# Up projections of a squared-ReLU MLP: a 512- and a 256-column matmul per weight tile against three of 256 columns

## The chip, the core and the metric

One NeuronCore of a Trainium2 chip runs the kernel. TensorE (PE) multiplies: it loads a stationary 128x128 tile (PEld in the profile) and streams a moving operand past it into PSUM, here in accumulators of one bank, 512 float32 columns. VectorE (DVE), ScalarE (ACT) and GpSimd (POOL) work beside it, and SyncE (SP) issues the weight transfers. The metric is the device time of one execution in microseconds; lower is better.

## What is computed

Two decoder layers over 256 tokens of width 2048, in float32. Layer 0 mixes tokens by differential attention, layer 1 by a gated linear recurrence; each is followed by a squared-ReLU MLP of hidden width 8192 and a gated per-layer embedding. The change touches the MLP:

```python
def sqrelu_mlp(xn, w_up, w_down):
    return jnp.square(jax.nn.relu(xn @ w_up)) @ w_down

for i in range(DEPTH):                                   # two layers
    h = h + mix                                          # attention or recurrence
    h = h + sqrelu_mlp(rmsnorm(h, g_mlp[i]), w_up[i], w_down[i])
    ple_gate = jax.nn.sigmoid(rmsnorm(h, g_ple[i]) @ w_ple_gate[i])
    h = h + ple_gate * (p[i] @ w_ple_proj[i])
```

## The kernel before

Every matrix product is made from float32 operands split into two float32r parts, `hi` and `lo`, and sums three of the four partial products: hi·hi, hi·lo and lo·hi. All products go through one weight stream, `stream(groups)`. A group is one product of [256 tokens, 512 columns] over `nk` k-tiles of 128. Its weights come in chunks of four k-tiles (one 1 MB transfer on SP's queue, three buffers); a chunk is cut into subs of two k-tiles, and each sub is split by one ACT cast (`w_hi`, L255) and one DVE subtraction (`w_lo`, L256) into one of four buffers, up to three subs ahead of the matmuls. Small work that hangs on a group (transposes, norms) is deferred by a number of subs and emitted between the matmuls.

In most groups the activations are stationary and 512 weight columns move: `mm3` (L249 to L251) issues three matmuls of 512 columns for each k-tile and each half of the tokens. The gate products of layer 1, the attention scores and the attention outputs use `mm3` too, with 256 or 128 moving columns.

The up projections of the MLP are transposed (`flip`): the result is wanted as [hidden, tokens], so a 128x128 weight tile is stationary and the 256 tokens move. The moving operand is a `Wide` tile (`x.both`), with the `hi` and the `lo` part of a k-tile side by side, 512 columns in all. For each weight tile (a k-tile `k`, one of four column blocks `f`) line L391 issues two matmuls. One has `w_hi` stationary and moves all 512 columns: columns 0 to 255 of the accumulator `acc[f]` receive hi·hi, columns 256 to 511 hi·lo. The other has `w_lo` stationary and moves the 256 `hi` columns into columns 0 to 255. So one group has four accumulators of a full bank, out of six in the pool. When the group is done, `up_evict` adds the two halves: an ACT copy of the right half (L644), a DVE addition (L645), then relu and square in one DVE instruction over two blocks (L646), and a split of the result into `big` tiles (L255, L256), the operand of the down projection.

One layer's MLP has 8 chunks of 1024 hidden columns. `up(c)` is two groups (2 x 16 k-tiles x 4 blocks = 128 weight tiles), `down(c)` four groups (4 x 8 k-tiles x 2 token halves x 3 = 192 matmuls of 512 columns). The order is up(0), up(1), down(0), up(2), down(1), and so on, so that a down projection never follows directly on the eviction that it needs, but for the last. Over both layers there are 16 x 128 = 2048 weight tiles.

Of the kernel before, what the change touches and what calls it, by code (L numbers as in the profile page):

```python
# [11 lines left out]
AF = mybir.ActivationFunctionType  # L12
# [30 lines left out]
class Chunk:  # L43
    """Up to KC k-tiles of one weight column block, moved by one DMA."""

# [5 lines left out]
class Sub:  # L51
    """SK k-tiles of a chunk, split into two float32r parts."""

# [6 lines left out]
class Group:  # L60
    """One product over nk k-tiles: [256 tokens, 512 columns], or its transpose where flip is set."""

# [11 lines left out]
def trunk_kernel(ctx: ExitStack, tc, a, out):  # L74
# [7 lines left out]
    def t4(shape, dtype=F32):  # L82
        """4 KiB a partition"""
        return wk.tile(shape, dtype, tag="t4", name="t4", bufs=3)
# [10 lines left out]
    def big(shape, dtype=F32):  # L95
        """8 KiB a partition"""
        return wk.tile(shape, dtype, tag="big", name="big", bufs=4)
# [12 lines left out]

# [1 line left out]
    state = {"tick": 0}  # L112
# [13 lines left out]

# [1 line left out]
    h = cp.tile([P, NT, D], F32, name="h")  # L128
# [66 lines left out]
    def lam_setup():  # L195
        """lambda of the differential attention, the same on every partition"""
        lamv = t2([P, 4, DK])
        for i, nm in enumerate(("lam_q1", "lam_k1", "lam_q2", "lam_k2")):
            nc.gpsimd.dma_start(lamv[:, i], a[nm][0].partition_broadcast(P))

        def finish():
            lamm = t1([P, 2, DK])
            nc.vector.tensor_tensor(lamm, lamv[:, 0::2], lamv[:, 1::2], op=ALU.mult)
            lams = sm.tile([P, 2], F32, name="lams", bufs=1)
            nc.vector.tensor_reduce(lams, lamm, axis=AX.X, op=ALU.add)
            lame = sm.tile([P, 2], F32, name="lame", bufs=1)
            nc.scalar.activation(lame, lams, AF.Exp)
            nc.vector.tensor_tensor(neg_lam, lame[:, 1:2], lame[:, 0:1], op=ALU.subtract)
            nc.vector.tensor_scalar(neg_lam, neg_lam, LAM0, None, op0=ALU.subtract)

        defer(4, finish)

    def mask_setup():
        """-(query - key) where the key is visible, else a huge negative number"""
        nc.gpsimd.iota(
            mtab, pattern=[[-P, NT], [1, SEQ]], base=0, channel_multiplier=-1, allow_small_or_imprecise_dtypes=True
        )
        nc.gpsimd.affine_select(
            mtab, mtab, pattern=[[P, NT], [-1, SEQ]], compare_op=ALU.is_ge, fill=NEG, base=0, channel_multiplier=1
        )  # L220

    # 8 * softplus(-lam): log1p(u) = 2 atanh(u / (2 + u)) with u = exp(-|lam|)
    sp8 = cp.tile([P, 16], F32, name="sp8")
# [22 lines left out]

# [1 line left out]
    def mm3(ps, lh, ll, rh, rl, start, stop):  # L248
# [4 lines left out]
    def split(hi, lo, src):  # L253
        """src = hi + lo exactly, each part of float32r's 12 significant bits."""
        nc.scalar.copy(hi, src)  # L255
        nc.vector.tensor_tensor(lo, src, hi.bitcast(F32), op=ALU.subtract)  # L256
# [5 lines left out]
    def rstd(ss, n, width, name):  # L262
        """(ss / width + EPS) ** -0.5 of [P, n]"""
        m = sm.tile([P, n], F32, name=name + "_m")
        nc.gpsimd.tensor_scalar(m, ss, 1.0 / width, EPS, op0=ALU.mult, op1=ALU.add)
        r = sm.tile([P, n], F32, name=name + "_r")
        nc.gpsimd.tensor_tensor(r, m, mhalf[:, :n], op=ALU.pow)
        return r

    def x32(shape):  # L270
        """32 KiB a partition"""
        return xp.tile(shape, F32R, tag="x32", name="x32")

    class Operand:
        """A split [k, token] operand of nk k-tiles."""

# [6 lines left out]
    class Wide(Operand):  # L283
        """Both parts of a k-tile side by side: one [k, 512] moving operand."""

# [4 lines left out]
    class Norm(Wide):  # L290
        """The rmsnorm of h as a transposed, split operand; the row factor r goes onto the products."""

# [37 lines left out]

# [1 line left out]
    def stream(groups):  # L332
# [34 lines left out]
        for g in groups:  # L367
            acc = [psum([P, NB]) for _ in range(4 if g.flip else NT)]
            kt = 0
            for i, s in enumerate(g.subs):  # L370
                load_to(cidx[id(s.chunk)] + W_RAW - 1)
                if i in g.pre:
                    g.pre[i](split_to)
                split_to(j + W_SPLIT - 1)
                j += 1
                if s.own is not None:
                    continue
                if g.flip:
                    x = g.lhs()
                    for f in range(4):  # L380
                        fs = slice(f * P, (f + 1) * P)
                        for kk in range(SK):
                            k = kt + kk
                            parts = [
                                (acc[f][:, :SEQ], s.lo[:, kk, fs], x.hi[:, k]),
                                (acc[f], s.hi[:, kk, fs], x.both[:, k].rearrange("p a t -> p (a t)")),
                            ]
                            if k == 0:
                                parts.reverse()
                            for n, (o, lh, rh) in enumerate(parts):  # L390
                                nc.tensor.matmul(  # L391
                                    o, lhsT=lh, rhs=rh, start=k == 0 and n == 0, stop=k == g.nk - 1 and n == 1
                                )
                else:
                    for t in range(NT):
                        for kk in range(SK):
                            k = kt + kk
                            lh, ll = g.lhs(k, t)
                            mm3(acc[t], lh, ll, s.hi[:, kk], s.lo[:, kk], k == 0, k == g.nk - 1)
                kt += SK  # L400
                state["tick"] += 1
                run_due()
            g.evict(acc)
# [3 lines left out]

# [1 line left out]
    pT = {}  # L409
# [14 lines left out]

# [1 line left out]
    n0 = Norm(G_MIX)  # L426
# [41 lines left out]
    def softmax(ps, heads, t, nk):  # L468
        """attn = softmax(c = 0) - lam * softmax(c = 1) of [P, heads, 2, nk] scores"""
        n = len(heads)  # L470
# [122 lines left out]
    def residual_evict(nb, norm, scale=None):  # L593
        """h += product; the last contribution to this block feeds the next norm."""

        def evict(acc):
            add_to_h(acc, nb, scale)
            if norm is not None:
                norm().feed(nb)

        return evict
# [22 lines left out]

# [1 line left out]
    FC = 1024  # L626
# [3 lines left out]
    def mlp(l, norm_in, norm_out):  # L630
        hid = {}

        def up_evict(c, half):
            """relu(.) ** 2 of a transposed product; the row factor squared goes onto the next product"""

            def evict(acc):
                if half == 0:
                    hid[c] = Operand(big([P, FKT, SEQ], F32R), big([P, FKT, SEQ], F32R))
                for b in range(2):
                    u = t2([P, 2, SEQ])  # L640
                    for i in range(2):
                        ps = acc[2 * b + i]
                        other = t1([P, SEQ])
                        nc.scalar.copy(other, ps[:, SEQ:])  # L644
                        nc.vector.tensor_tensor(u[:, i], ps[:, :SEQ], other, op=ALU.add)  # L645
                    nc.vector.scalar_tensor_tensor(u, in0=u, scalar=0.0, in1=u, op0=ALU.max, op1=ALU.mult)  # L646
                    ks = slice(half * 4 + 2 * b, half * 4 + 2 * b + 2)
# [24 lines left out]

# [1 line left out]
    def ple(l, norm_in, norm_out):  # L674
# [49 lines left out]

# [1 line left out]
    w_in = a["w_in_rec"][0]  # L726
# [9 lines left out]
    def gate_weights():  # L736
        """They lie in the k-tiles of yT that come last."""
        w = yT().both[:, 8:16]
        return w[:, :, 0], w[:, :, 1]
# [64 lines left out]
    def recur(half):  # L804
        """a = exp(-s r), b = sqrt(1 - a^2) i x with 1 - a^2 = tanh(s r) (1 + a^2); then the scan"""

# [66 lines left out]
    def gate_chunk(nb):  # L873
        """The gate weights of 512 channels: they go through the weight stream's loads and splits."""
        ch = Chunk(None, KC)
# [34 lines left out]

    # the first group takes x as it comes
    first = groups[0]
# [64 lines left out]
```

## Time and profile before

| | us |
|---|---|
| median of 3 runs | 2328.12 |
| lowest and highest of them | 2327.57 and 2328.15 |
| span of the profiled execution | 2326.8 |
| PE busy | 2308.8 (99%) |
| DVE busy, ACT busy | 1424.6 (61%), 1193.6 (51%) |
| matmuls, and weight loads | 11467 each |

The span runs from the first to the last instruction of the profiled execution. It is 1.3 us below the median. Matmuls are pipelined: the duration of one (0.28 us with 256 columns) is longer than the distance to the next, so what a matmul occupies is read from the distance between two starts, or from a stretch of known length divided by the count of matmuls in it. "This matmul's pace" below means that distance.

### The profile page before, as it was taken

How to read it: one execution, taken by the hardware profiler on the slowest of the kernel's cores; microseconds unless marked ns; L12 is line 12 of the kernel's file. 1: busy time of each engine (PE TensorE's matmuls, PEld its weight loads, DVE VectorE, ACT ScalarE, POOL GpSimd, SP SyncE). 2: the span in 40 equal slices, each digit the busy share in tenths (PEclk: the TensorE clock that was granted, in tenths of full speed). 3: DMA queues.
4: the chain of work that ended last, by engine and by line, in shares of the span. 5: the costliest groups of instructions: out<-in, count | busy, mean ns of one | idle time of the engine just before them, and what ended most of it. 6: DMA issues, size and time to landing. Idle time of an engine off the chain costs nothing.

```text
span 2326.8 us, 28564 instructions
## 1 busy us (share of the span) xinstructions
PE 2308.8 (99%) x11467; PEld 1946.9 (84%) x11467; DVE 1424.6 (61%) x1704; ACT 1193.6 (51%) x1594; POOL 44.7 (2%) x79
## 2 busy tenths in 40 slices
PE   8999999999999999999999999999999999999999
PEld 6888888888888888888888887888888888888887
DVE  6676655565565665566566767566565555565654
ACT  6555554444444444444558887454444444444453
POOL 2100000000000000000000000000000000000000
PEclk9999999999999999999999999999999999999999
DMA  7454555555565655655566565556565565555554
GB/s 241 163 185 163 165 179 181 185 195 189 191 197 184 198 188 192 196 185 181 189 193 219 187 212 181 181 182 198 184 197 190 191 197 184 198 189 191 177 199 148
DMA packets 225396, 438.95 MB, mean 189 GB/s; under 512 B 7582, under 2 KB 16416, under 8 KB 225264
## 3 DMA queue, kind: packets, MB, share of 16 engines
q1 hardware_dynamic: 224608, 436.24, 57.3%
q8 instruction: 89, 1.46, 0.3%
q0 software_dynamic: 608, 0.89, 0.2%
q14 instruction: 43, 0.35, 0.0%
q10 hardware_dynamic: 48, 0.02, 0.0%
HBM read 435.01 MB, written 2.10 MB: 188 GB/s over the span
## 4 chain that ended last, share of the span: by engine, by line
PE 94%; DVE 2%; ACT 2%; DMA 1%; issue 1%; SPq 0%; POOL 0%; DVEq 0%; ACTq 0%
PE acc L391 31%; PE acc L251 21%; PE acc L249 20%; PE acc L250 20%; PE tp L317 1%; DVE w_lo L256 1%; ACT w_hi L255 1%; DMA w_raw<-in_w_gate_x_dram 0%; DVE t L770 0%; DMA h<-in_x_dram 0%; PE tp L458 0%; DVE big L827 0%; ACT L810 0%; SPq L351 0%; ACT L788 0%
## 5 line engine op out<-in xcount | busy, mean ns | idle before, releaser
L256 DVE TENSOR_TENSOR w_lo<-w_raw,w_hi 128x1024 fp32r<-128x1024 f32 x808 | 987.4, 1224 | 781.4 <-ACT w_hi L255 779.9
L255 ACT CAST w_hi<-w_raw 128x1024 fp32r<-128x1024 f32 x808 | 849.0, 1052 | 979.8 <-PE acc L251 605.7
L391 PE MATMUL acc<-x,w_hi 128*128 128x512 f32 x2048 | 704.8, 394 | 0.0
L391 PE MATMUL acc<-x,w_lo 128*128 128x256 f32 x2048 | 547.8, 278 | 0.0
L249 PE MATMUL acc<-w_hi,x 128*128 128x512 f32 x1152 | 457.1, 397 | 0.0
L250 PE MATMUL acc<-w_lo,x 128*128 128x512 f32 x1152 | 450.2, 391 | 1.9 <-DVE w_lo L256 1.8
L251 PE MATMUL acc<-w_hi,x 128*128 128x512 f32 x1152 | 450.5, 391 | 0.0
L391 PEld LDWEIGHTS acc<-x,w_hi 128*128 128x128 f32 x2048 | 376.0, 188 | 78.6
L249 PE MATMUL acc<-w_hi,big 128*128 128x512 f32 x1024 | 399.7, 390 | 0.0
L251 PE MATMUL acc<-w_hi,big 128*128 128x512 f32 x1024 | 398.6, 389 | 0.0
L250 PE MATMUL acc<-w_lo,big 128*128 128x512 f32 x1024 | 398.4, 389 | 0.0
L391 PEld LDWEIGHTS acc<-x,w_lo 128*128 128x128 f32 x2048 | 384.7, 188 | 11.2
L251 PEld LDWEIGHTS acc<-w_hi,x 128*128 128x128 f32 x1152 | 216.8, 188 | 46.8 <-DVE x L256 0.2
L250 PEld LDWEIGHTS acc<-w_lo,x 128*128 128x128 f32 x1152 | 217.2, 189 | 45.0 <-DVE w_lo L256 3.0
L249 PEld LDWEIGHTS acc<-w_hi,x 128*128 128x128 f32 x1152 | 216.8, 188 | 41.7
L251 PEld LDWEIGHTS acc<-w_hi,big 128*128 128x128 f32 x1024 | 192.2, 188 | 40.3
L250 PEld LDWEIGHTS acc<-w_lo,big 128*128 128x128 f32 x1024 | 192.3, 188 | 39.8
L249 PEld LDWEIGHTS acc<-w_hi,big 128*128 128x128 f32 x1024 | 192.2, 188 | 39.0
L589 DVE SCALAR_TENSOR_TENSOR h<-acc,n_r,h 128x512 f32<-128x512 f32 x128 | 89.9, 744 | 0.0
L644 ACT COPY t<-acc 128x256 f32<-128x256 f32 x128 | 47.5, 371 | 22.8 <-PE acc L391 20.6
L259 ACT ACTIVATE x<-tp,cols_a 128x256 fp32r<-128x256 f32 (+1 forms) x72 | 35.7, 496 | 39.5 <-DVE x L260 39.5
L260 DVE SCALAR_TENSOR_TENSOR x<-tp,cols_a,x 128x256 fp32r<-128x256 f32 (+1 forms) x72 | 36.8, 511 | 18.8 <-ACT x L259 18.8
(173 smaller groups left out, 1064.2 us busy)
## 6 DMA issues: line engine op xcount, KB each, us to landing
w_raw<-in_w_up_dram SPq DMA_DIRECT2D x128, 1024.0 KB, 5.2
w_raw<-in_w_down_dram SPq DMA_DIRECT2D x128, 1024.0 KB, 5.1
w_raw<-in_w_qkv_dram SPq DMA_DIRECT2D x47, 1024.0 KB, 5.2
w_raw<-in_w_ple_gate_dram SPq DMA_DIRECT2D x32, 1024.0 KB, 5.2
w_raw<-in_w_in_rec_dram SPq DMA_DIRECT2D x32, 1024.0 KB, 5.5
w_raw<-in_w_o_attn_dram SPq DMA_DIRECT2D x16, 1024.0 KB, 5.2
w_raw<-in_w_o_rec_dram SPq DMA_DIRECT2D x16, 1024.0 KB, 5.1
w_raw<-in_w_ple_proj_dram SPq DMA_DIRECT2D x8, 512.0 KB, 3.7
```

Source lines behind the costliest of these rows:

```text
L249: nc.tensor.matmul(ps, lhsT=lh, rhs=rh, start=start, stop=False)
L250: nc.tensor.matmul(ps, lhsT=lh, rhs=rl, start=False, stop=False)
L251: nc.tensor.matmul(ps, lhsT=ll, rhs=rh, start=False, stop=stop)
L255: nc.scalar.copy(hi, src)
L256: nc.vector.tensor_tensor(lo, src, hi.bitcast(F32), op=ALU.subtract)
L259: nc.scalar.activation(hi, src, AF.Copy, scale=scale)
L260: nc.vector.scalar_tensor_tensor(lo, in0=src, scalar=scale, in1=hi.bitcast(F32), op0=ALU.mult, op1=ALU.subtract)
L317: nc.tensor.transpose(tp[:, i, t * P : (t + 1) * P], h[:, t, (k0 + i) * P : (k0 + i + 1) * P], ident)
L391: nc.tensor.matmul(o, lhsT=lh, rhs=rh, start=k == 0 and n == 0, stop=k == g.nk - 1 and n == 1)
L589: nc.vector.scalar_tensor_tensor(hb, in0=acc[t], scalar=scale()[:, t : t + 1], in1=hb, op0=ALU.mult, op1=ALU.add)
L644: nc.scalar.copy(other, ps[:, SEQ:])
```

## The change

In flip groups each weight tile gets three matmuls of 256 columns: `w_hi` with the `hi` tokens, `w_hi` with the `lo` tokens, `w_lo` with the `hi` tokens, all three into the same 256 columns. Two column blocks share one bank (`acc[f // 2][:, f % 2]`), so a group has two accumulators in place of four. Only the first matmul into a bank carries the start flag. The eviction has no halves to add: ACT applies relu to both blocks of a bank at once, and DVE multiplies that by the accumulator. The diff also drops comments and docstrings, which is not shown; L391 becomes L392, and L644 to L646 become L643 and L644.

```diff
-            acc = [psum([P, NB]) for _ in range(4 if g.flip else NT)]
+            acc = [psum([P, 2, SEQ]) if g.flip else psum([P, NB]) for _ in range(NT)]
...
                     for f in range(4):
                         fs = slice(f * P, (f + 1) * P)
+                        o = acc[f // 2][:, f % 2]
                         for kk in range(SK):
                             k = kt + kk
                             parts = [
-                                (acc[f][:, :SEQ], s.lo[:, kk, fs], x.hi[:, k]),
-                                (acc[f], s.hi[:, kk, fs], x.both[:, k].rearrange("p a t -> p (a t)")),
+                                (s.hi[:, kk, fs], x.hi[:, k]),
+                                (s.hi[:, kk, fs], x.lo[:, k]),
+                                (s.lo[:, kk, fs], x.hi[:, k]),
                             ]
-                            if k == 0:
-                                parts.reverse()
-                            for n, (o, lh, rh) in enumerate(parts):
+                            for n, (lh, rh) in enumerate(parts):
                                 nc.tensor.matmul(
-                                    o, lhsT=lh, rhs=rh, start=k == 0 and n == 0, stop=k == g.nk - 1 and n == 1
+                                    o, lhsT=lh, rhs=rh, start=k == 0 and n == 0 and f % 2 == 0,
+                                    stop=k == g.nk - 1 and n == 2, skip_group_check=True,
                                 )
...
                 for b in range(2):
                     u = t2([P, 2, SEQ])
-                    for i in range(2):
-                        ps = acc[2 * b + i]
-                        other = t1([P, SEQ])
-                        nc.scalar.copy(other, ps[:, SEQ:])
-                        nc.vector.tensor_tensor(u[:, i], ps[:, :SEQ], other, op=ALU.add)
-                    nc.vector.scalar_tensor_tensor(u, in0=u, scalar=0.0, in1=u, op0=ALU.max, op1=ALU.mult)
+                    nc.scalar.activation(u, acc[b], AF.Relu)
+                    nc.vector.tensor_tensor(u, u, acc[b], op=ALU.mult)
```

On PE, where the first up projection of layer 0 follows the last matmuls of the attention's output projection, the program before has these instructions (`x_2943` is the normed, split input of the MLP, `x_2244` the attention output):

```order
L250 MATMUL acc<-w_lo,x_2244 128x512
L251 MATMUL acc<-w_hi,x_2244 128x512
L391 MATMUL acc<-x_2943,w_hi 128x512
L391 MATMUL acc<-x_2943,w_lo 128x256 x2
L391 MATMUL acc<-x_2943,w_hi 128x512 x2
```

And the changed one, at the same place:

```order
L250 MATMUL acc<-w_lo,x_2244 128x512
L251 MATMUL acc<-w_hi,x_2244 128x512
L392 MATMUL acc<-x_2943,w_hi 128x256 x2
L392 MATMUL acc<-x_2943,w_lo 128x256
L392 MATMUL acc<-x_2943,w_hi 128x256 x2
```

The last two rows of each repeat from there on: per weight tile one matmul of 512 and one of 256 columns before, three of 256 now. The places of the groups among one another are the same.

On ACT, at the end of the first up group, the eviction before (`t_3635` and `t_3645` are the two work tiles, `t_3636` to `t_3649` the copied halves):

```order
L255 CAST w_hi<-w_raw 128x1024 x5
L644 COPY t_3636<-acc 128x256
L644 COPY t_3639<-acc 128x256
L644 COPY t_3646<-acc 128x256
L644 COPY t_3649<-acc 128x256
L255 CAST w_hi<-w_raw 128x1024
L255 CAST big<-t_3635 128x512
L255 CAST w_hi<-w_raw 128x1024
L255 CAST big<-t_3645 128x512
```

And in the changed program:

```order
L255 CAST w_hi<-w_raw 128x1024 x5
L643 ACTIVATE t_3697<-acc 128x512
L255 CAST w_hi<-w_raw 128x1024
L255 CAST big<-t_3697 128x512
L643 ACTIVATE t_3702<-acc 128x512
L255 CAST w_hi<-w_raw 128x1024
L255 CAST big<-t_3702 128x512
```

Four copies of 256 columns became two relus of 512, and the weight casts (`w_hi`) that stood behind all four now stand one behind each relu.

## Rows read from the trace of the kernel before

**Rows 1.** The page: busy time, granted clock in 40 slices, chain that ended last.

```profile
PE 2308.8 (99%) x11467; PEld 1946.9 (84%) x11467; DVE 1424.6 (61%) x1704; ACT 1193.6 (51%) x1594; POOL 44.7 (2%) x79
...
PEclk9999999999999999999999999999999999999999
...
PE 94%; DVE 2%; ACT 2%; DMA 1%; issue 1%; SPq 0%; POOL 0%; DVEq 0%; ACTq 0%
PE acc L391 31%; PE acc L251 21%; PE acc L249 20%; PE acc L250 20%; PE tp L317 1%; DVE w_lo L256 1%; ACT w_hi L255 1%; DMA w_raw<-in_w_gate_x_dram 0%; DVE t L770 0%; DMA h<-in_x_dram 0%; PE tp L458 0%; DVE big L827 0%; ACT L810 0%; SPq L351 0%; ACT L788 0%
```

**Rows 2.** The chain in order of time: start us, us, what; three up stretches.

```profile
410.34 83.64 PE acc L391 x480
537.50 44.40 PE acc L391 x256
...
1649.24 44.40 PE acc L391 x256
```

**Rows 3.** Who waited for whom: us in total, times, longest us.

```profile
ACT w_hi L255 <- PE acc L391: 350.8, 218, 1.8
...
ACT t L644 <- PE acc L391: 20.6, 64, 0.3
```

**Rows 4.** Busy by stretch: one down(c), then one up(c); us and (xinstructions).

```profile
493.97:537.50 43.53, 43.53 (x194) 36.04 (x193) 27.16 (x30) 18.29 (x19) 0.00 (x0) 1.00 0.59 192
537.50:581.90 44.40, 44.40 (x258) 38.80 (x257) 24.63 (x28) 20.28 (x25) 0.00 (x0) 1.00 0.59 192
```

**Rows 5.** The page's groups: up matmuls, and loads of L249 and L250.

```profile
L391 PE MATMUL acc<-x,w_hi 128*128 128x512 f32 x2048 | 704.8, 394 | 0.0
L391 PE MATMUL acc<-x,w_lo 128*128 128x256 f32 x2048 | 547.8, 278 | 0.0
...
L250 PEld LDWEIGHTS acc<-w_lo,x 128*128 128x128 f32 x1152 | 217.2, 189 | 45.0 <-DVE w_lo L256 3.0
L249 PEld LDWEIGHTS acc<-w_hi,x 128*128 128x128 f32 x1152 | 216.8, 188 | 41.7
```

**Rows 6.** Timeline of PE in layer 1: a gate product, 256 columns, stationary weights.

```profile
1252.72 0.28 PE L249 MATMUL acc<-v,x 128*128 128x256 f32 x1
...
1254.13 0.39 PE L249 MATMUL acc<-w_hi,x 128*128 128x512 f32 x1
```

**Rows 7.** Timeline of PE in the attention: scores with 256 columns.

```profile
80.44 0.28 PE L251 MATMUL acc<-x 128*128 128x256 f32 x1
...
80.92 0.40 PE L249 MATMUL acc<-w_hi,x 128*128 128x512 f32 x1
```

**Rows 8.** Timeline of PE in the attention: output product, 256 columns, behind transposes.

```profile
242.36 0.28 PE L250 MATMUL acc<-v,big 128*128 128x256 f32 x1
...
243.61 0.39 PE L249 MATMUL acc<-w_hi,x 128*128 128x512 f32 x1
```

**Rows 9.** Timeline of PE in the attention: scores with 128 columns.

```profile
76.14 0.28 PE L250 MATMUL acc<-x 128*128 128x128 f32 x1
...
77.26 0.28 PE L251 MATMUL acc<-x 128*128 128x128 f32 x1
```

**Rows 10.** Groups of ACT and DVE at evictions: busy us, mean ns, idle before.

```profile
L644 ACT COPY t<-acc 128x256 f32<-128x256 f32 x128 | 47.5, 371 | 22.8 <-PE acc L391 20.6
L435 ACT ACTIVATE t<-acc,n_r 128x512 f32<-128x512 f32 x16 | 10.9, 684 | 1.9 <-PE acc L251 1.5
...
L645 DVE TENSOR_TENSOR t<-acc,t 128x256 f32<-128x256 f32 x128 | 47.9, 416 | 0.0
L646 DVE SCALAR_TENSOR_TENSOR t<-t 128x512 f32<-128x512 f32 x64 | 43.6, 682 | 0.0
...
L587 DVE TENSOR_TENSOR h<-h,acc 128x512 f32<-128x512 f32 x16 | 10.2, 680 | 0.0
```

**Rows 11.** Timeline of ACT at the end of an up group.

```profile
559.74 0.37 ACT L644 COPY t<-acc 128x256 f32<-128x256 f32 x1 [0.32 <-PE acc L391]
560.00 1.06 ACT L255 CAST w_hi<-w_raw 128x1024 fp32r<-128x1024 f32 x1
...
565.30 1.05 ACT L255 CAST w_hi<-w_raw 128x1024 fp32r<-128x1024 f32 x1 [1.10 <-PE acc L391]
```

## Prediction

> **What bounds the kernel now.** Read first the busy shares and the chain that ended last [rows 1]. PE is busy 99% of the span and carries 94% of the chain; the up matmuls of L391 alone carry 31% of it. The granted clock is full in all 40 slices. Read next the chain in order of time [rows 2]: an up(c) is one unbroken piece of 44.40 us with 256 matmuls of L391 and nothing of another engine in it. There are six such pieces a layer, and before them one of 83.64 us with 480 matmuls, which is most of up(0) and up(1). Then the list of waits [rows 3]: where L391 stands there, it is the one waited for. ACT's weight casts wait 350.8 us for it, because they run ahead and want a free buffer, and no row has PE waiting in the MLP. So in the up stages PE's own pace is the time, and a matmul added or shortened there moves the end by what it adds or saves. The up stages are where the change acts; DVE is busy 24.63 of 44.40 us there and ACT 20.28 [rows 4].
>
> **What PE pays per weight tile before.** One up(c) is 128 weight tiles in 44.40 us [rows 4], so a tile costs 44.40 / 128 = 346.9 ns, for one matmul of 512 and one of 256 columns. One down(c) is 192 matmuls of 512 columns in 43.53 us [rows 4], so one of 512 columns takes 226.7 ns. If the 512-column matmul of an up tile costs the same, the 256-column one beside it costs 346.9 - 226.7 = 120.2 ns, which is more than half of 226.7 (113.4). Read as a price per column and one per matmul, 512 columns at 226.7 and 256 at 120.2 differ by 106.5 ns, so 256 columns cost 106.5 ns and every matmul, with the load that goes with it, costs 13.7 ns beside. The work in columns is 768 a tile before and after; what the change adds is one more matmul and one more load a tile.
>
> **Does every matmul have a load of its own?** Yes by the page's counts: L249 and L250 run one behind the other with the same stationary tile and still have 1152 loads each [rows 5]. So the two matmuls with `w_hi` will load it twice, and PE goes from two loads and two matmuls a tile to three and three.
>
> **The price of three.** The first estimate is 3 x 120.2 = 360.6 ns a tile, 13.7 more than 346.9. The trace has three other places with runs of 256-column matmuls, each with its own load. The gate products are the closest in form: stationary weights, moving activations, three matmuls a tile, half a bank as accumulator. From 1252.72 to 1254.13 there are 12 steps in 1.41 us, 117.5 ns each [rows 6], so a tile would cost 352.5, 5.6 more. The scores move a tile from the same kind of buffer as the up stage: 4 steps from 80.44 to 80.92, 120.0 ns [rows 7]. An attention output product that starts right behind transposes shows 11 steps from 242.36 to 243.61, 113.6 ns [rows 8]. So the extra per tile lies between -6.1 ns (3 x 113.6 = 340.8) and +13.7 ns, with the two steady cases at +5.6 and +13.1. I take +13.7, because it comes from the very tiles in question (`w_hi` and `w_lo` stationary, `x` moving, in the same buffers) and the scores agree with it; the gates and the output products move a tile of another pool. Halving the columns again does not go much lower: with 128 columns 10 steps from 76.14 to 77.26 take 112 ns each [rows 9]. That row says that below some width the load, and no longer the columns, sets the pace, and 256 columns are already near it. It speaks against a cheap third matmul.
>
> Sum on PE: 2048 tiles x 13.7 ns = +28.1 us; at the gates' pace 2048 x 5.6 = +11.5 us.
>
> The Trainium skill bears on this, and against the rows ("TensorE: Matmul & The Clock Gate", section Back-to-back issue gap): at full clock the gap is the columns divided by 2.4 GHz plus 2.5 ns, and weight loads are given no share in that formula. By it the extra matmul would cost 2.5 ns a tile, an estimate of 5 us in all. The 226.7 ns of a 512-column step [rows 4] stand against the 215.8 that it gives, so here the row decides.
>
> **The rest of the change, on ACT and DVE.** Per up group ACT drops four copies of 371 ns and gains two relus of 512 columns out of PSUM, for which the nearest row is an ACT pass over 128x512 out of PSUM, 684 ns [rows 10]: 1.48 us against 1.37. DVE drops four additions of 416 ns and two passes of 682 ns, 3.03 us, and gains two multiplications of 128x512 with one operand in PSUM, nearest row 680 ns: 1.36 us [rows 10]. Both engines idle half of the stage, and nobody on the chain waits for them, so I cost the 1.7 us that DVE saves per group at nothing. The cover is PE's own stretch: an up group lasts 22.2 us, and the split tiles are read by a down projection that starts a whole up(c) later. Only behind the last chunk of each layer does down(6) alone, 43.5 us, lie between; that covers it too. The new order puts a weight cast behind each relu, where before the casts stood behind all four copies. The first relu waits for two blocks, the second for all four, so the second is released where the fourth copy was, by 559.74 in the stretch shown, and the next cast began at 560.00; the one at 565.30 waited 1.10 us for a buffer that PE still held [rows 11]. The casts run against the buffers, not against PE. The two casts behind the relus start at most a relu's length later than now, and the buffers are three subs (8.3 us) ahead, so this too costs nothing; if that cover were gone it would be under a microsecond in each of 32 groups. The accumulators take two banks of six in place of four, so no group waits for a bank that it did not wait for before. Transfers and SP's queue keep their order and have more time.
>
> **Sum.** The profiled execution has a span of 2326.8 us and the median of the runs is 1.3 us above it. 2326.8 + 28.1 = 2354.9 by span, and 2356 as the median. With the gates' pace it is 2326.8 + 11.5 + 1.3 = 2339.6. About 0.2% (4.7 us) is what a measurement of this kernel can tell from no change.
>
> **The rivals.**
> First, faster: PE settles in the 113.6 ns rhythm of the output product [rows 8]. A tile then costs 340.8 and the kernel 2048 x 6.1 = 12.5 us less, 2315.6. It decides as soon as the pace is under 346.9 / 3 = 115.6 ns. For it: that row exists, and its stationary and moving tiles look like any others. Against: it stands only behind transposes, and the up stages follow 512-column matmuls, as the gates and scores of [rows 6, 7] do. 5%.
> Second, little change: the third matmul costs almost nothing beside its columns, a pace of 115 to 116.4 ns and a time of 2323.5 to 2332.8. For it: the split into a price per column and one per matmul rests on a subtraction, and some of the 13.7 ns may belong to columns. Against: no steady row lies in that gap. 6%. The page's formula above is the same idea at +2.5 ns a tile, 2048 x 2.5 = 5.1 us and 2333.2, just outside; as a mechanism of this kernel it needs a pace of 116.5 ns, which no row shows. 3%.
> Third, much slower: PE cannot be fed that fast for long. Before, an up stage takes four PE instructions in 346.9 ns, 86.7 ns each; now six in 360.6, 60.1 each. The rows show such a rate (112 / 2 = 56 ns in [rows 9]) for 12 matmuls at a time, never for the 384 of an up(c). If the steady rate of instructions were 65 ns, a tile would cost 390 and the kernel 2048 x 43 = 88 us more, 2416. It decides from 60 ns on. For it: nothing in the trace bounds the rate in a long run under 86.7. Against: no step in the bursts lengthens towards their end. 8%.
> That the change does not do what it says (the second load of `w_hi` is left out) is excluded as far as the counts of [rows 5] go; I give it nothing of its own.
>
> **How the numbers follow.** The forecast, slower by the extra load and matmul at a pace between 117.5 and 120.2 ns, has 78%: 2339.6 to 2356.1, with the upper end likelier. The range widens this by 4 us below and 8 us above, for a pace some ns off and for a wait or two at the evictions: 2336 to 2364. Outside it lie the rivals, 22% before counting that the range's edges take in a little of them. Faster by over 0.2%: 5%. Within 0.2%: 6%. Slower by over 0.2%: 78 + 3 + 8 = 89%.
>
> **What would show it.** In the profile after, an up(c) stretch in the chain should be one piece of 46.2 us (45.1 at the gates' pace) with 384 matmuls, and the down stretches should still take 43.5. Starts of the up matmuls should lie 120 ns apart throughout, with PE waiting for nobody. If the stretch is 43.6 us, the first rival holds; if it is 48 us or more with no waits, the third. If ACT or DVE appears in the chain inside the MLP, my claim that the eviction is covered is wrong.

## The result, and the profile after

The changed kernel takes 2353.65 us (median of 4 runs, 2352.7 to 2353.88), against 2327.85 us for the kernel before in the same comparison (2327.08 to 2328.15). The ratio is 1.011, with a 95% interval of 1.0095 to 1.0124: 25.8 us, 1.1% slower. The forecast was 2356, with a range of 2336 to 2364.

The page of the changed kernel has PE at 99% of the span, as before [rows 1], but with 2048 more matmuls and loads (13515 for 11467) and with 25.7 us more of PE's time, while DVE and ACT have less to do:

```profile
span 2350.9 us, 32627 instructions
...
PE 2334.5 (99%) x13515; PEld 2062.4 (88%) x13515; DVE 1384.3 (59%) x1576; ACT 1182.4 (50%) x1530; POOL 44.6 (2%) x79
...
PEclk9999999999999999999999999999999999999999
```

The chain in order of time, layer 1, whose pieces answer to [rows 2] (start us, us, what):

```profile
1526.50 2.87 PE acc L392 x24
1529.81 2.88 PE acc L392 x24
1533.12 86.39 PE acc L392 x720
1663.06 46.07 PE acc L392 x384
1752.67 46.07 PE acc L392 x384
```

An up(c) is still one unbroken piece of PE, now 46.07 us for 44.40, with 384 matmuls for 256: 120.0 ns each, 359.9 a tile for 346.9. The busy times by stretch answer to [rows 4]; the first is a down(c), the second the up(c) behind it, in the same columns (us, then PE, PEld, DVE, ACT, POOL, and behind them the granted clock, the share of the DMA engines and GB/s):

```profile
495.39:538.94 43.55, 43.55 (x195) 36.06 (x194) 25.68 (x27) 18.39 (x19) 0.00 (x0) 1.00 0.58 189
538.94:585.01 46.07, 46.07 (x386) 46.07 (x384) 23.61 (x23) 19.49 (x21) 0.00 (x0) 1.00 0.57 187
```

The down stretch takes 43.55 us for 43.53, unchanged. In the up stretch a weight load is now in flight all the time, 46.07 of 46.07 us for 38.80 of 44.40 before: with a load under every 256 columns no moment is left without one. The granted clock is 1.00 in both stretches, as before, so it has no part in the difference.

What the stages gained adds up. In each layer the 240 tiles of the first long piece went from 83.64 to 86.39 us (+2.75), six up(c) from 44.40 to 46.07 (+1.67 each), and the 16 tiles between the first transposes from 2.78 + 2.80 to 2.87 + 2.88 (+0.17; read for before in layer 0). That is 12.9 us a layer and 25.9 for both, against 25.8 between the medians. The spans of the two profiled executions differ by 24.1. Of the 1.8 us between, 1.3 lie ahead of the first up matmul, which started at 403.7 us and now at 402.4, in a part of the program that is the same in both; I take that for scatter between executions.

### The profile page after: what moved, and what is told of

It reads as the page before. It is cut to its first block, busy times and chain, and to the rows that moved or that the text cites. A ratio compares the mean times of both kernels' runs of the same rounds, so it can differ in the third digit from the quotient of the medians.

```text
span 2350.9 us, 32627 instructions
## 1 busy us (share of the span) xinstructions
PE 2334.5 (99%) x13515; PEld 2062.4 (88%) x13515; DVE 1384.3 (59%) x1576; ACT 1182.4 (50%) x1530; POOL 44.6 (2%) x79
## 5 line engine op out<-in xcount | busy, mean ns | idle before, releaser
L392 PE MATMUL acc<-x,w_hi 128*128 128x256 f32 x4096 | 738.2, 283 | 0.0
L392 PEld LDWEIGHTS acc<-x,w_hi 128*128 128x128 f32 x4096 | 640.2, 192 | 1.1
L392 PE MATMUL acc<-x,w_lo 128*128 128x256 f32 x2048 | 580.2, 283 | 0.0
L249 PE MATMUL acc<-w_hi,x 128*128 128x512 f32 x1152 | 457.3, 397 | 0.0
L250 PE MATMUL acc<-w_lo,x 128*128 128x512 f32 x1152 | 450.0, 391 | 1.4 <-DVE w_lo L256 1.3
L249 PE MATMUL acc<-w_hi,big 128*128 128x512 f32 x1024 | 400.1, 391 | 0.0
L250 PE MATMUL acc<-w_lo,big 128*128 128x512 f32 x1024 | 398.8, 389 | 0.0
L392 PEld LDWEIGHTS acc<-x,w_lo 128*128 128x128 f32 x2048 | 393.5, 192 | 0.0
L250 PEld LDWEIGHTS acc<-w_lo,x 128*128 128x128 f32 x1152 | 217.1, 188 | 44.2 <-DVE w_lo L256 2.5
L249 PEld LDWEIGHTS acc<-w_hi,x 128*128 128x128 f32 x1152 | 216.8, 188 | 41.6 <-ACT x L259 0.3
L251 PEld LDWEIGHTS acc<-w_hi,big 128*128 128x128 f32 x1024 | 192.3, 188 | 40.2
L249 PEld LDWEIGHTS acc<-w_hi,big 128*128 128x128 f32 x1024 | 192.4, 188 | 39.1
L250 PEld LDWEIGHTS acc<-w_lo,big 128*128 128x128 f32 x1024 | 192.4, 188 | 39.0
L643 ACT ACTIVATE t<-acc 128x512 f32<-128x512 f32 x64 | 38.1, 595 | 16.4 <-PE acc L392 16.4
```

Source lines behind the costliest of these rows:

```text
L249: nc.tensor.matmul(ps, lhsT=lh, rhs=rh, start=start, stop=False)
L250: nc.tensor.matmul(ps, lhsT=lh, rhs=rl, start=False, stop=False)
L251: nc.tensor.matmul(ps, lhsT=ll, rhs=rh, start=False, stop=stop)
L392: nc.tensor.matmul(o, lhsT=lh, rhs=rh, start=k == 0 and n == 0 and f % 2 == 0, stop=k == g.nk - 1 and n == 2, skip_group_check=True,)
L643: nc.scalar.activation(u, acc[b], AF.Relu)
```

## The experiments

My theory: the extra load and matmul on PE, at 120 ns for each 256-column matmul, are the whole of the 25.8 us. The rivals were a share of the eviction or of the two-bank accumulators, a price that depends on which tile is loaded, and the gates' pace of 117.5 ns, whose cause the prediction had left open.

### Three short matmuls with the old accumulators and the old eviction

```diff
-                                (acc[f][:, :SEQ], s.lo[:, kk, fs], x.hi[:, k]),
-                                (acc[f], s.hi[:, kk, fs], x.both[:, k].rearrange("p a t -> p (a t)")),
+                                (acc[f][:, :SEQ], s.hi[:, kk, fs], x.hi[:, k]),
+                                (acc[f][:, SEQ:], s.hi[:, kk, fs], x.lo[:, k]),
+                                (acc[f][:, :SEQ], s.lo[:, kk, fs], x.hi[:, k]),
...
```

> The kernel before with one thing changed: the 512-column matmul of an up tile is two of 256, into the left and the right half of the old full-bank accumulator. Four accumulators a group and the old eviction stay. My theory (the third load and matmul on PE are the whole of it, 120 ns each): an up(c) of 46.1 us with 384 matmuls, and 2328 + 2048 x 13.1 ns = 2354.7, the same as the changed kernel within 1.5 us. Rival (the shared bank or the lighter eviction gives or takes a part): the up(c) differs from 46.07 us or the time differs from 2353.7 by 3 us or more.

Measured 2353.59 us (2353.16 to 2354.15), ratio to before 1.0111 (1.0094 to 1.0128). In the chain of this kernel the up stretches are those of the changed kernel:

```profile
409.36 86.39 PE acc L390 x720
539.30 46.07 PE acc L390 x384
```

So splitting the 512-column matmul alone brings the whole loss, and the shared banks and the lighter eviction bring nothing. The edit allocates no tile anew, so the loss does not come from tiles that lie elsewhere in SBUF either, which will matter below.

### A heavier eviction

```diff
                     nc.scalar.activation(u, acc[b], AF.Relu)
+                    for _ in range(2):
+                        nc.scalar.copy(u, u)
+                        nc.vector.tensor_scalar_mul(u, u, 1.0)
                     nc.vector.tensor_tensor(u, u, acc[b], op=ALU.mult)
```

> The changed kernel with extra work in the eviction: two more ACT copies and two more DVE passes by 1.0 over each 128x512 relu, 8 instructions a group, some 2.5 us of ACT and 1.4 to 2.7 us of DVE in each of 32 groups. My theory (the eviction is covered by PE's stretch): no change, 2353.7 within 1.5 us, no ACT or DVE in the chain inside the MLP. Rival (the lighter eviction was worth something on the path): up to 32 x 2.5 = 80 us more, and a gap between an up group and the next matmuls.

Measured 2353.91 us (2352.79 to 2354.2), the same as the changed kernel. The added groups of ACT and DVE (busy us, mean ns, idle before):

```profile
L645 ACT COPY t<-t 128x512 f32<-128x512 f32 x128 | 79.2, 619 | 2.0
L646 DVE TENSOR_SCALAR t<-t 128x512 f32<-128x512 f32 x128 | 54.0, 422 | 17.2 <-ACT t L645 17.2
```

79 us more of ACT and 54 us more of DVE, and the up(c) stays at 46.07 us. The eviction is covered with much to spare; that is why making it cheaper could not pay for anything.

### Another order of the three

```diff
                                 (s.hi[:, kk, fs], x.hi[:, k]),
-                                (s.hi[:, kk, fs], x.lo[:, k]),
                                 (s.lo[:, kk, fs], x.hi[:, k]),
+                                (s.hi[:, kk, fs], x.lo[:, k]),
```

> The changed kernel with the three matmuls of a tile in the order hi.hi, lo.hi, hi.lo, so that no two neighbours in a tile share the stationary tile. My theory (each matmul pays for a load of its own, the same one or not): 120.0 ns each, 46.07 us an up(c), 2353.7 within 1.5 us. Rival (loading the same tile again is cheaper or dearer than another): the price of a third of the matmuls changes; 5 ns would be 2048 x 5 = 10 us either way.

Measured 2353.38 us (2352.82 to 2355.03), an up(c) of 46.07 us in its chain. A second load of the tile that is already loaded is neither cheaper nor dearer than a load of another.

### A fourth matmul, and six of 128 columns

```diff
+                                (s.lo[:, kk, fs], x.lo[:, k]),
...
```

> The changed kernel with a fourth matmul of 256 columns a tile, lo.lo, which adds the partial product that the others leave out. My theory (a price per matmul, PE paces the stage): 4 x 120.0 ns a tile, 61.4 us an up(c) for 46.07, 2048 x 120.0 = +245.8 us, 2599. Rival (the engine has room beside the three): less than that. Rival (instructions cannot be supplied that fast for long): the pace rises over 120 ns in the longer runs.

Measured 2601.34 us in one run; the chain has up stretches of 512 matmuls:

```profile
570.65 61.43 PE acc L393 x512
```

That is 120.0 ns each again, and 247.7 us more than the changed kernel's median, where 245.8 was expected. The price is per matmul, and there is no room beside the three.

```diff
-                                nc.tensor.matmul(
-                                    o, lhsT=lh, rhs=rh, ...
+                                for t in range(NT):
+                                    ts = slice(t * P, (t + 1) * P)
+                                    nc.tensor.matmul(
+                                        o[:, ts], lhsT=lh, rhs=rh[:, ts], ...
```

> The changed kernel with each 256-column matmul cut into two of 128 columns, six a tile, the same columns in all. Theory A (a price per column and one of 13.6 ns per matmul): 53.2 + 13.6 = 66.8 ns each, 401 a tile, 2048 x 41 = +84 us, 2438. Theory B (the load sets a floor of 112 ns, as in the runs of twelve scores): 672 a tile, 2048 x 312 = +639 us, 2993. Rival (the supply of instructions fails in a run of 768): over 112 ns each and over 2993.

Measured 2987.83 us in one run. Its chain has an up(c) in one piece:

```profile
2060.02 85.71 PE acc L394 x768
```

85.71 / 768 = 111.6 ns for a matmul of 128 columns: theory B, as in [rows 9], now in runs of 768. The price per column and per matmul, which gave 66.8 ns, is wrong at this width: half the columns cost 111.6 ns for 120.0. No run has a width under 128 columns or between 128 and 256, so where the price stops to follow the columns is not shown. The third rival of the prediction is excluded by the same row. A load and a matmul in 111.6 ns are 55.8 ns an instruction, held over 1536 instructions, and the changed kernel asks for one in 60.0.

### The down projections split in the same way

```diff
-                            mm3(acc[t], lh, ll, s.hi[:, kk], s.lo[:, kk], k == 0, k == g.nk - 1)
+                            for n, (st, mv) in enumerate(((lh, s.hi), (lh, s.lo), (ll, s.hi))):
+                                for c in range(2):
+                                    cs = slice(c * SEQ, (c + 1) * SEQ)
+                                    nc.tensor.matmul(acc[t][:, cs], lhsT=st, rhs=mv[:, kk, cs], ...
```

(in the groups of eight k-tiles alone)

> The kernel before with its up stage untouched; in the down projections (activations stationary, weights moving) each 512-column matmul is two of 256 with the same stationary tile, 6144 short ones for 3072 long ones. My theory (256 columns cost 120 ns in a long run wherever they stand): 240.0 in place of 226.7, a down(c) of 46.1 us for 43.5, 3072 x 13.3 = +41 us, 2369. Rival (the gates' pace holds where weights or a tile of another pool move): 235.0, +25 us, 2353. Rival (the output products' 113.6): 227.2, no change.

Measured 2367.71 us (2367.54 to 2368.56), ratio 1.0172 (1.0155 to 1.0189): 40.2 us more than the 2327.54 of the kernel before in that comparison, where 41 was expected. The chain has a down(c) and the up(c) behind it:

```profile
493.48 46.06 PE acc L405 x384
539.54 44.42 PE acc L391 x256
```

46.06 / 384 = 119.95 ns. With the roles changed over (activations stationary, weights moving) the price is the same: 240 ns for two halves, 226.7 for the whole.

### The layout of the moving tile

```diff
-            self.both = x32([P, KT_D, 2, SEQ])
-            self.hi, self.lo = self.both[:, :, 0], self.both[:, :, 1]
+            self.both = x32([P, 2, KT_D, SEQ])
+            self.hi, self.lo = self.both[:, 0], self.both[:, 1]
...
```

(the gate weights, which lie in a tile of the same kind, are indexed accordingly)

> The changed kernel with the moving tile laid out as all hi tokens and then all lo tokens, so that a matmul's 256 columns lie at steps of 1 KB as those of the gate products do, and no longer at steps of 2 KB. Theory A (120 ns is what a 256-column matmul costs behind its like, whatever the address): 46.07 us an up(c), 2353.7 within 1.5 us. Theory B (the 117.5 ns of the gates comes from where the moving tile lies): 45.1 us an up(c), 2.5 x 6144 = 15 us less, 2338.

Measured 2353.21 us (2352.7 to 2353.95), an up(c) of 46.07 us, as theory A had it. The step between k-tiles is not what makes the gates faster; that no address matters, as theory A says further, does not follow from it and falls below.

### Longer runs of gate products

The split down projections seemed to begin their runs at 117.5 ns (four steps in 0.47 us) and then to keep 120 (six in 0.72), on the timeline of PE, though 0.01 us is the last digit of these rows:

```profile
583.79 0.40 PE L405 MATMUL acc<-w_hi,big 128*128 128x256 f32 x2
...
584.26 0.64 PE L405 MATMUL acc<-w_hi,big 128*128 128x256 f32 x4
...
584.98 0.64 PE L405 MATMUL acc<-w_hi,big 128*128 128x256 f32 x4
```

So perhaps the gates' 12 matmuls only end before they settle. In this kernel each gate product is issued four times over.

```diff
-                        mm3(ps[:, g], gh[:, e, js], gl[:, e, js], xch[:, 2 * n + k], xcl[:, 2 * n + k], k == 0, k == 1)
+                        for again in range(4):
+                            mm3(ps[:, g], gh[:, e, js], gl[:, e, js], xch[:, 2 * n + k], xcl[:, 2 * n + k], ...)
```

> The changed kernel with each gate product of layer 1 issued four times over into the same accumulator (the sums are four times the reference's), so that a run of 12 matmuls of 256 columns, 117.5 ns apart, becomes one of 48. Theory A (a run starts a little faster and settles at 120 ns wherever its tiles lie, as the split down projections showed within ten matmuls): the last 30 of each run lie 120.0 ns apart. Theory B (the pace belongs to the tiles, weights of one pool and activations of another): 117.5 ns to the end. The time itself grows by 16 x 36 x 0.12 = 69 us at most, less where PE waited there anyway: 2353 to 2423.

Measured 2417.64 us in one run. Theory A, my own, falls. The second run of 48, from its first matmul to the first behind it, on the timeline:

```profile
1268.55 0.28 PE L249 MATMUL acc<-v,x 128*128 128x256 f32 x1
...
1274.20 0.39 PE L249 MATMUL acc<-w_hi,x 128*128 128x512 f32 x1
```

48 steps in 5.65 us, 117.7 ns to the end. Theory B, that the pace belongs to the tiles, does not hold either. The very first run starts behind transposes and has another pace:

```profile
1260.59 0.28 PE L251 MATMUL acc<-v,x 128*128 128x256 f32 x1
...
1265.81 0.39 PE L249 MATMUL acc<-w_hi,x 128*128 128x512 f32 x1
```

46 steps in 5.22 us, 113.5 ns, to the end of the run. The first run of the next four gate products reads, by the program, from the same SBUF buffers, but starts behind a 512-column matmul, and it ran at 117.7 again (48 steps from 1305.53 to 1311.18). In this kernel a run keeps the pace in which it starts.

### Other places in SBUF

The same kernel with the four large pools allocated in the opposite order, so that only addresses change.

```diff
-    wraw = ctx.enter_context(tc.tile_pool(name="wraw", bufs=W_RAW))
-    wsp = ctx.enter_context(tc.tile_pool(name="wsp", bufs=W_SPLIT))
-    xp = ctx.enter_context(tc.tile_pool(name="xp", bufs=2))
     wk = ctx.enter_context(tc.tile_pool(name="wk", bufs=2))
+    xp = ctx.enter_context(tc.tile_pool(name="xp", bufs=2))
+    wsp = ctx.enter_context(tc.tile_pool(name="wsp", bufs=W_SPLIT))
+    wraw = ctx.enter_context(tc.tile_pool(name="wraw", bufs=W_RAW))
```

> The kernel with the gate products issued four times over, and the four large pools laid out in SBUF in the opposite order (work tiles, wide operands, split weights, raw weights), so that every stationary and moving tile lies at another address; the instructions are the same. Theory C (the rhythm of a run, 120.0 ns in the up stage and 117.8 in the gates, comes from where the tiles lie): at least one of the two, or the 226.8 ns of 512 columns, changes by more than 1 ns; an up(c) that ran at 117.8 would take 45.2 us, and all of them at it 13 us less. Theory D (it comes from something else in the runs): 120.0, 117.8 and 226.8 as they were, and 2418 within 3 us.

Measured 2439.43 us in one run, 21.8 more than the kernel above. The up stretch and the down stretch behind it:

```profile
540.67:586.72 46.05, 46.05 (x385) 46.05 (x384) 23.52 (x23) 19.50 (x21) 0.00 (x0) 1.00 0.55 186
586.72:631.53 44.81, 44.81 (x195) 36.10 (x193) 25.78 (x27) 18.32 (x19) 0.00 (x0) 1.00 0.58 186
```

The up stage kept its 120 ns, but a down(c) went from 43.55 to 44.81 us, 233.4 ns a matmul for 226.8, without any wait of PE; sixteen such differences are 20.2 of the 21.8 us. The gate run behind transposes went from 113.5 to 120.0 ns (25 steps in 3.00 us), and the second from 117.7 to 119.8 (48 in 5.75):

```profile
1271.12 0.28 PE L249 MATMUL acc<-v,x 128*128 128x256 f32 x1
...
1274.12 0.28 PE L250 MATMUL acc<-v,x 128*128 128x256 f32 x1
...
1278.91 0.28 PE L249 MATMUL acc<-v,x 128*128 128x256 f32 x1
...
1284.66 0.40 PE L249 MATMUL acc<-w_hi,x 128*128 128x512 f32 x1
```

So theory C holds in this: where the tiles lie moves the pace of a matmul, here by 2 to 6%. It also decides whether a start behind transposes leaves a faster rhythm, as it did above and does not here.

### The moving tile in the work tiles' place

The changed kernel with the moving operand copied by ACT into the tiles that the gate products move from, and then the kernel before with the same copy (its two matmuls a tile kept).

```diff
+                if g.flip:
+                    def fetch(n):
+                        if n * SK < g.nk:
+                            xv[n] = v4([P, SK, 2, SEQ], F32R)
+                            nc.scalar.copy(xv[n], g.lhs().both[:, n * SK : (n + 1) * SK])
+                    if i == 0:
+                        xv = {}
+                        fetch(0)
+                    fetch(i + 1)
...
```

> The changed kernel with the moving operand of the up stage copied, two k-tiles ahead by one more ACT pass a sub, into the work tiles from which the gate products and the attention's output products move theirs. Theory C (the place of the moving tile sets 117.8 against 120.0): 117.8 ns, 45.2 us an up(c), 2048 x 3 x 2.2 = 13.5 us less, 2340. Theory D (it does not): 120.0 ns, 46.07 us, 2353.7, provided that ACT's copies, 1.05 us in a sub of 2.9 us beside a cast of 1.05, keep ahead of PE.

Measured 2332.87 us in one run, 20.8 less than the changed kernel's median, and with 267 us more of ACT. The chain in one up(c) (start us, us, what):

```profile
624.49 22.51 PE acc L403 x191
...
649.09 0.94 ACT v L376
650.03 0.04 issue
650.07 19.32 PE acc L403 x168
```

The first piece runs at 22.51 / 191 = 117.9 ns, and the last, behind a copy that came some 0.3 us late, at 19.32 / 168 = 115.0 in the mean, most of it at 113.3:

```profile
650.53 0.39 PE L403 MATMUL acc<-v,w_hi 128*128 128x256 f32 x2
...
652.91 0.28 PE L403 MATMUL acc<-v,w_hi 128*128 128x256 f32 x1
```

(21 steps in 2.38 us). A short wait of PE left it in a faster rhythm, which won back in the rest of the group more than the wait had cost. This kernel changes the place of the moving tile and adds the copies at the same time, so it does not separate the two.

> The kernel before, with its two matmuls a tile, and with the moving operand copied two k-tiles ahead by one ACT pass a sub into the work tiles. Theory C: the 256-column matmul at 113.3 to 117.7 ns and the 512-column one at 226.7, 340 to 344 a tile for 346.9: 43.5 to 44.1 us an up(c), 2314 to 2323, less some 0.3 us where a copy comes late in a group. Theory D: 346.9 a tile, 2328, or more by what the copies hold up.

Measured 2338.0 us (2337.75 to 2338.24), ratio 1.0044 (1.0027 to 1.0061): slower than before, where 5 to 14 us less was expected. The last kernel moves nothing but a pool, the one that holds the moving tile, with the instructions of the kernel before:

```diff
-    xp = ctx.enter_context(tc.tile_pool(name="xp", bufs=2))
     wk = ctx.enter_context(tc.tile_pool(name="wk", bufs=2))
+    xp = ctx.enter_context(tc.tile_pool(name="xp", bufs=2))
```

> The kernel before, instructions and all, with one pool moved in SBUF: the wide operands (the moving tile of the up stage, and its neighbours) lie behind the work tiles, at the far end, no longer between the split weights and the work tiles. Theory C (where the tiles lie sets a part of the pace, and the far end is the better place): an up tile of 340 to 344 ns for 346.9, an up(c) of 43.5 to 44.1 us for 44.40, 5 to 14 us less over both layers, 2314 to 2323, if no other stage pays for it. Theory D (the gain of the copied operand came from something else, such as the waits that the copies brought): 44.40 us an up(c) and 2328 within 2 us.

Measured 2343.64 us (2343.36 to 2344.46), ratio 1.0068 (1.0053 to 1.0083), again a miss of the 2314 to 2323 that was expected. In both kernels an up(c) takes 45.12 us for 44.40, first in the kernel with the moved pool, then in the one with the copy:

```profile
539.53 45.12 PE acc L391 x256
```

```profile
1654.08 45.12 PE acc L401 x256
```

45.12 / 128 = 352.5 ns a tile for 346.9. The far end, where three short matmuls gained 2 to 7 ns each, costs the pair of a long and a short one 5.6. So that the place matters is shown, by the moved pool above all, and my reading of which place is the better one is refuted. Of the kernels run, the kernel before stays the fastest.

Between the two kernels with the copy, the change has the other sign: three short matmuls take 2332.87 us (one run) against 2338.0 for the pair, 5.1 us less, and the up(c) shown above lasts 44.90 us (624.49 to 669.39) against 45.12. By the paces, three at 117.9 ns are 353.7 a tile and at 113.3 they are 340, against the pair's 352.5. The evictions differ too, but that is worth nothing by the first two experiments. The 25.8 us are therefore the price of the third matmul in this layout, and no fixed price of a load and a matmul.

## Why the prediction was right

**What bounds the kernel.** Right. PE's pace was the time of the up stages, and nothing else entered the chain there before or after. The profile of the changed kernel has the one piece per up(c) that was named as the sign, 46.07 us for 46.2, and down stretches of 43.55 for 43.5.

**A load for each matmul.** Right: the loads grew with the matmuls, from 11467 to 13515.

**The price of three.** Right in kind and nearly in size, but the number came in part by luck. The subtraction gave 120.2 ns for the 256-column matmul of the old pair, on the condition that the 512-column one beside it costs 226.7 as in a down step, and the pace of three is 120.0. The starts in the kernel before say that the condition did not hold:

```profile
562.32 0.28 PE L391 MATMUL acc<-x,w_lo 128*128 128x256 f32 x1
562.44 0.39 PE L391 MATMUL acc<-x,w_hi 128*128 128x512 f32 x1
562.67 0.27 PE L391 MATMUL acc<-x,w_lo 128*128 128x256 f32 x1
```

The short one has 0.12 us to the next start and the long one 0.23; in the mean over the up(c) of [rows 4] it is 115.8 and 230.8 ns (some 110 steps each that the timeline shows singly). So the tiles in question, read by their starts, gave a pace of 116 ns, and three of them 347 a tile: the second rival. The sentence against that rival, that no steady row lies between 115 and 116.4, was wrong, and the split into 106.5 ns for the columns and 13.7 for a matmul and its load rested on the same condition. Of the reasons given for 120 rather than 117.5, only the scores [rows 7] remain, and four steps are a thin base; the same 120.0 appears with tiles of other pools too, as in the split down projections, and with the operand copied elsewhere the pace changed.

The sum was 28.1 us, the stages gained 25.9, and two terms make the difference. One is the 0.2 ns a step, 0.7 a tile, 1.4 us. The other is that 346.9 ns was put on all 2048 tiles, while the 240 tiles of each layer's first long piece took 83.64 / 240 = 348.5 [rows 2]; they had less to lose, 2 x 240 x 1.6 ns = 0.8 us. The row had been quoted, but not divided.

**The formula of the Trainium skill.** The Trainium skill ("TensorE: Matmul & The Clock Gate", section Back-to-back issue gap) gives 109.2 ns for 256 columns and 55.8 for 128 at full clock, as the gap of an isolated matmul. The measured 120.0 and 111.6 differ from it, so the rows decided rightly, and at 128 columns its price per column does not hold for matmuls that each bring a load.

**The eviction at nothing.** Right, and shown by adding work to it. The relu took 595 ns for the 684 of the nearest row, the multiplication 680 for 680; neither mattered:

```profile
L643 ACT ACTIVATE t<-acc 128x512 f32<-128x512 f32 x64 | 38.1, 595 | 16.4 <-PE acc L392 16.4
```

```profile
L644 DVE TENSOR_TENSOR t<-t,acc 128x512 f32<-128x512 f32 x64 | 43.5, 680 | 0.0
```

**The rivals.** The 113.6 ns rhythm did not come in this kernel, but the argument against it was only half right. It is not bound to transposes: with the moving tile in another place PE fell into it after a wait of 0.3 us, and with it three short matmuls cost 340 ns a tile, less than the pair before. The second rival did not come either, though the starts above spoke for it: three short matmuls in a row, with no long one among them, run at 120.0 ns here, while the short ones between long ones ran at 115.8. The third rival, that PE cannot be fed so fast, is excluded by the run of 128-column matmuls.

**What stays open.** Why a 256-column matmul with its load takes 113.3, 117.7 or 120.0 ns. The runs show that it depends on where the tiles lie and on how the run starts, and that in the changed kernel the step between k-tiles and the order of the loads don't matter. At 113.3 ns a short matmul costs half of a down step's 226.7, so in that rhythm the additional load is free. Which relation of addresses decides, and why the place that suits three short matmuls costs the pair 5.6 ns, no run here tells.

## What to carry to other kernels

Where PE is the chain, count matmuls and their loads beside columns: here a 512-column matmul cut in two costs 240 ns for 226.7, and one of 128 columns costs with its load 111.6, nearly as much as one of 256. Check a price that comes from a subtraction against the starts in the trace: here it gave 120.2 ns for a matmul that the starts have at 115.8, and only a run of the new shape elsewhere had the pace that came. Such a run bounds the price and does not fix it, since the same change costs 25.8 us in one layout and gains 5.1 in another. An eviction on engines that idle half of the stage had no price to trade for PE's time, however much lighter it got.

## What the hardware showed that I had not expected

The place of the tiles in SBUF moves PE's pace with the same instructions and no wait: a down(c) by 2.9% when the pools changed order (43.55 to 44.81 us), the whole kernel by 0.7% when one pool moved (2327.8 to 2343.6 us). A run of short matmuls also kept the rhythm in which it started, 117.7 or 113.5 ns over 48 matmuls from the same buffers, and after a wait of 0.3 us the rest of a group ran faster, at 113.3 ns for 117.9; with the pools in the other order no faster rhythm came behind the transposes. Whoever compares two kernels to a percent has to look whether their buffers lie in the same places.
